# A new order for the mixers' steps and units in a two-layer hybrid backbone

## The chip, the cores and the metric

One core of a Trainium2 chip runs the whole program. The metric is device microseconds of one execution; the time given is the median of three.

## What is computed

One step of a two-layer backbone, for 128 context tokens and 256 latent tokens (T = 384 columns) of width 1024. Each layer projects its normed input `h` into the inputs of four mixers, weighs each mixer's projected output with sigmoid gates, adds the four, and goes on to an output projection and an MLP:

```python
h = _rms(x, norm_g[l, 0]) * (1.0 + sc1) + sh1
z = h @ w_in[l]
ya, ckv, kr = _mla(za, ...)            # A: latent attention
yb = _chunk_mlp(zb, ...)               # B: gated unit over chunks of 128 positions
yc, st = _mlstm(zc, ...)               # C: the cell, a matrix memory read in both directions
yd, kd, vd = _diff_attn(zd, ...)       # D: differential attention
br = jnp.einsum('blnw,nwd->blnd', jnp.stack([ya, yb, yc, yd], axis=2), w_branch[l])
gates = jax.nn.sigmoid(h @ w_merge[l] + b_merge[l]).reshape(B, L, N_BRANCH, D_MODEL)
y = jnp.sum(gates * br, axis=2) @ w_out[l]
```

In the cell the head outputs are normed and multiplied with another sigmoid:

```python
h = _rms(h, head_norm.reshape(H_C, DH_C)).reshape(B, L, D_C)
out = (jax.nn.sigmoid(o.astype(jnp.float32)) * h).astype(z.dtype)
```

## The kernel before

Activations lie with channels on the 128 partitions and the 384 tokens in the columns. Every large weight comes in blocks of 128 by 1024 and is split into two parts of fewer bits: `whi` by a cast on ScalarE (L117), `wlo` by a subtraction on VectorE (L119). The inputs are split the same way, into `hh` and `hl`. A *unit* is the work with one weight block on TensorE: 24 matmuls of 384 columns (`mm3`, L350 to L352) in most units, 36 of 256 columns in those that compute values with tokens on the partitions (`vproj`, L403 to L405). Results go to PSUM, which has four tiles called `mm` for units and four called `px` for everything smaller; each pool gives its tiles out in turn, so that a new use waits until the last reader of the old one is done.

`mix_plan` lists the units of a layer's mixing part in the order of their weights: five units for the cell's queries, keys and gate rows (MISC), two for the gated unit's `u` (BU), then values of the cell (CV), values of the gated unit (BV), the cell's output gate (CO), queries and keys of D (DQ, DK), and then four branches. A branch has twice four merge units (M0 to M7), whose sigmoids make the gates on ScalarE, and a branch unit (BR00 and BR01 in branch 0) after each four. The branch unit multiplies the mixer's output with its weights; VectorE multiplies four result blocks with the gates and, from the second branch on, adds them to `acc` (L1103 to L1106). Between branch 0 and branch 1 stand the values of D (DV) and the inputs of A (AQ, AKV). In layer 0 no work of a previous layer runs into this part. In layer 1 the part before it, here called the head, has computed the first units while it was still norming and scaling its input; `zb` and `zs` (L1543, L1544) are its results copied out of PSUM.

The mixers themselves are generators. `slot()` stands ahead of every unit: it orders loads and casts, runs each living generator as far as its next `yield` (`pump`), and then issues the due `wlo` subtractions and the jobs kept for that index. So the order on each engine is the order in which Python writes it, and every engine works through its own queue in that order. A generator is started by `spawn`; `finish` runs one to its end, which is what a branch does with its mixer before its branch unit. `C` is the cell (`mlstm`, L765), `B` the gated unit (`gmlp`, L746), `D` differential attention (`diff`), `A0` and `A` latent attention.

Names that the steps use: L775 are the cell's first products, which transpose the gate rows `grow` made by L1033. L411 spreads rows of the split operands `zq` and `mts` over partitions. L919 to L922 read the cell; L950 makes its new state; L966 sums squares for its last norm, L427 to L439 and L970, L971 are that norm's steps on VectorE. L754 are the gated unit's products, which read `qi`. In D, L642 are the scores, L601 and L602 the maximum and its scaling, L647 to L650 the weights of the softmax, L571 their transposes. L1172 and L1179 sum squares for A's norms.

Of the kernel before, what the change touches and what calls it, by code (L numbers as in the profile page):

```python
# [40 lines left out]
class Builder:  # L41
# [704 lines left out]
    def gmlp(self, l, vn, ub, wst, vb):  # L746
        nc = self.nc
        yh, yl = self.y_tiles(1)
        for b in range(2):
# [15 lines left out]
    def mlstm(self, l, grow, qc, km, kp, so):  # L765
# [96 lines left out]
        mask0()  # L862
        yield

        hbuf = s1([128, 2, T], "s3")
# [68 lines left out]
        for b in range(2):  # L934
            prev = None
            for hf in range(2):
                for d in range(2):
                    heads(b, hf, d, prev)
                    prev = (hf, d)
                    yield  # L940
            read(b, 0, prev)
            yield
            read(b, 1, None)
            if b == 0:
                nc.gpsimd.dma_start(self.c0, io["c0"][l, :, :, 1])
            yield
        for d in range(2):
            ps = self.px_tile()
# [26 lines left out]
    @staticmethod  # L975
    def mix_plan():
        w = lambda a, n: list(range(a, a + n))
        o = w(U_MISC, 5) + w(U_BU, 2) + w(U_CV, 2) + w(U_BV, 2) + w(U_CO, 2)
        for n in range(4):
            if n == 0:  # L980
                o += w(U_DQ, 4)
            if n == 1:
                o += w(U_DV, 5)
            for p in range(2):
                o += w(U_MERGE + 8 * n + 4 * p, 4) + w(U_BR + 2 * n + p, 1)
        return o

    def mix_phase(self, l, head):
# [60 lines left out]
        for j in range(len(head.units), len(fns)):  # L1049
            fns[j][0](fns[j][1], self.fm(l, self.mix_plan()[j], hh, hl), None)  # L1050
        for t, ps in enumerate(self.vproj(l, U_CV, hh, hl)):
            nc.scalar.copy(self.vcx[:, t].rearrange("p b (q e) -> p b q e", e=64)[:, :, 0:3:2, :],
                           ps.rearrange("p (b q e) -> p b q e", b=2, e=64))
        so = s1([128, 2, T], "s3")
        self.spawn("C", self.mlstm(l, grow, qc, km, kp, so))

# [10 lines left out]
        self.spawn("B", self.gmlp(l, vn, ub, wst, vb))  # L1067
        for b, ps in self.fm_pair(l, U_CO, hh, hl):
            self.sigmoid(so[:, b, :], ps)

        acc = self.hp.tile([128, KC, T], F32, tag="acc", name="acc")

        def branch(n, name):
            br = BR_ORDER[n]
            for part in range(2):
                gates, held = [], []
                for b in range(4 * part, 4 * part + 4):
                    held.append((b, self.fm(l, U_MERGE + n * 8 + b, hh, hl)))
                    if b % 2:
                        for bb, ps in held:  # L1080
                            g = mx.tile([128, T], F32, tag="g", name="g", bufs=4)
                            self.sigmoid(g, ps, bias=par[:, P_BM + br * 8 + bb:P_BM + br * 8 + bb + 1])
                            gates.append(g)
                        held = []
                self.finish(name)
                yh, yl = self.y[br]
# [10 lines left out]
                for j in range(4):  # L1097
# [4 lines left out]
                    if n == 0:  # L1102
                        nc.vector.tensor_tensor(acc[:, b, :], ps[:, :T], gates[j], ALU.mult)  # L1103
                    else:
                        nc.vector.tensor_tensor(gates[j], ps[:, :T], gates[j], ALU.mult)
                        nc.vector.tensor_tensor(acc[:, b, :], acc[:, b, :], gates[j], ALU.add)  # L1106
                    if end:
                        nc.scalar.copy(mh[:, b, 0:T], acc[:, b, :])
                        for k in late:
                            nc.vector.tensor_tensor(ml[:, k, 0:T], acc[:, k, :], mh[:, k, 0:T].bitcast(F32), ALU.subtract)  # L1110
                        late = [b]
                        if j == 1:
                            self.prefetch(len(self.split_w) + 1)
                if end:
                    nc.vector.tensor_tensor(ml[:, b, 0:T], acc[:, b, :], mh[:, b, 0:T].bitcast(F32), ALU.subtract)
                    self.low_parts()
            if n == 3:
                return mh, ml
# [18 lines left out]
        for b in range(2):  # L1137
# [5 lines left out]
            self.spawn("R", operand(self.kscr, b, kd, "ks", 512))  # L1143
        branch(0, "B")

        vd = s1([128, 4, 256], "vd")
        dma(vd[:, 1, :], io["xdv"][l])

        for t, ps in enumerate(self.vproj(l, U_DV, hh, hl)):
            nc.scalar.copy(vd[:, (0, 2, 3)[t], :], ps)  # L1150
        nc.gpsimd.dma_start(io["o_dv"][l], vd[:, 0, :])
        self.spawn("D", self.diff(l, stacks, vd))

# [15 lines left out]
        def latent():  # L1169
            ss = self.px_tile()  # L1170
            for i in range(2):
# [4 lines left out]
            for i in range(2):  # L1176
                nc.vector.scalar_tensor_tensor(zq[i], zq[i], par[:, P_QN + i:P_QN + i + 1], rs, ALU.mult, ALU.mult)
            ss = self.px_tile()
            nc.tensor.matmul(ss[:, :T], self.ones, sqk, start=True, stop=True)  # L1179
# [551 lines left out]
```

## Time and profile before

| | |
|---|---|
| median of three runs | 1407.64 us (1407.39 to 1408.38) |
| the profiled execution | 1410.98 us, its span 1409.2 us |
| TensorE busy | 1345.1 us, 95% of the span |
| VectorE busy | 943.1 us, 67% |
| ScalarE busy | 750.4 us, 53% |
| chain that ended last | TensorE 79%, VectorE 11%, ScalarE 5% |
| mixing part of layer 0, of layer 1 | 64 to 395 us, 764 to 1070 us |

The profile's "idle" is time in which an engine had nothing to run, with the instruction that ended it. TensorE's idle time is what the program could lose or win; idle time of the others costs nothing by itself. TensorE's clock has two levels here, 2.4 GHz (1.00 in the rows) and 1.2 GHz (0.50).

### The profile page before, as it was taken

Reading aid. Unit: us, or ns where it says so; the run is one execution under the profiler, and the core shown is the slowest. Engines: PE = TensorE matmul, PEld = TensorE weight load, DVE = VectorE, ACT = ScalarE, POOL = GpSimd, SP = SyncE. Lnnn points to the kernel's source line nnn. Section 1 sums busy time; section 2 is a strip of 40 time slices with the busy share of each in tenths; the row PEclk is TensorE's granted clock in tenths of the full one; section 3 lists DMA queues with packets and bytes.
Section 4 is the critical chain, followed back from the end, with each engine's and each line's share of the span. In section 5 each row is a group of like instructions: output and inputs, shape, how many; then the busy total and the mean of one; then the engine's idle time right before and its main releaser. Section 6 shows DMA issues by size and latency. Waiting matters only on the chain.

```text
span 1409.2 us, 20419 instructions
## 1 busy us (share of the span) xinstructions
PE 1345.1 (95%) x7722; PEld 1256.7 (89%) x7722; DVE 943.1 (67%) x1831; ACT 750.4 (53%) x1378; POOL 68.9 (5%) x128
## 2 busy tenths in 40 slices
PE   5999998999999999999999899899999999999995
PEld 2888887887998999999979899898989899999995
DVE  5557767865556777898777877786655676236544
ACT  4544756756455662264357467576745565235431
POOL 0101111100000000000001020210000000000000
PEclk9999999999999999999999999999999999999998
DMA  9355546445253447766745363542434443433331
GB/s 377 125 180 164 167 146 172 127 135 209 90 175 125 165 144 230 232 214 198 251 153 187 98 168 103 139 126 90 158 96 165 135 135 118 132 125 120 120 105 45
DMA packets 63090, 216.38 MB, mean 154 GB/s; under 512 B 7888, under 2 KB 11152, under 8 KB 62608
## 3 DMA queue, kind: packets, MB, share of 16 engines
q1 hardware_dynamic: 51552, 187.53, 40.2%
q0 software_dynamic: 10288, 25.51, 6.4%
q10 hardware_dynamic: 1152, 2.04, 0.4%
q8 instruction: 61, 1.00, 0.3%
q14 instruction: 37, 0.30, 0.1%
HBM read 207.27 MB, written 7.77 MB: 153 GB/s over the span
## 4 chain that ended last, share of the span: by engine, by line
PE 79%; DVE 11%; ACT 5%; issue 4%; DMA 1%; POOL 0%; SPq 0%; DVEq 0%; ACTq 0%; POOLq 0%
PE mm L350 22%; PE mm L351 22%; PE mm L352 22%; PE px L281 2%; DVE wlo L119 2%; PE mm L403 1%; ACT whi L117 1%; PE px L463 1%; PE mm L405 1%; PE mm L404 1%; DVE s L926 1%; PE px L589 1%; ACT L69 1%; PE px L727 1%; DVE yr L490 1%
## 5 line engine op out<-in xcount | busy, mean ns | idle before, releaser
L350 PE MATMUL mm<-hh,whi 128*128 128x384 f32 (+1 forms) x1344 | 469.8, 350 | 5.5 <-ACT hh L1505 2.9
L351 PE MATMUL mm<-hl,whi 128*128 128x384 f32 (+1 forms) x1344 | 458.5, 341 | 1.8 <-DVE hl L1510 1.8
L352 PE MATMUL mm<-hh,wlo 128*128 128x384 f32 (+1 forms) x1344 | 457.1, 340 | 0.0
L117 ACT CAST whi<-raw 128x1024 fp32r<-128x1024 f32 x268 | 279.2, 1047 | 259.8 <-PE mm L351 143.6
L119 DVE TENSOR_TENSOR wlo<-raw,whi 128x1024 fp32r<-128x1024 f32 x268 | 325.1, 1221 | 136.8 <-ACT whi L117 136.4
L350 PEld LDWEIGHTS mm<-hh,whi 128*128 128x128 f32 x1344 | 255.8, 190 | 31.7 <-issue 13.6
L351 PEld LDWEIGHTS mm<-hl,whi 128*128 128x128 f32 x1344 | 256.1, 191 | 5.2 <-DVE hl L1510 2.3
L352 PEld LDWEIGHTS mm<-hh,wlo 128*128 128x128 f32 x1344 | 255.9, 190 | 0.1
L351 PE MATMUL mm<-fl,whi 128*128 128x384 f32 x512 | 173.0, 338 | 0.0
L352 PE MATMUL mm<-fh,wlo 128*128 128x384 f32 x512 | 172.6, 337 | 0.0
L350 PE MATMUL mm<-fh,whi 128*128 128x384 f32 x512 | 172.4, 337 | 0.0
L352 PEld LDWEIGHTS mm<-fh,wlo 128*128 128x128 f32 x512 | 96.2, 188 | 0.0
L350 PEld LDWEIGHTS mm<-fh,whi 128*128 128x128 f32 x512 | 96.2, 188 | 0.0
L351 PEld LDWEIGHTS mm<-fl,whi 128*128 128x128 f32 x512 | 96.2, 188 | 0.0
L338 DVE SCALAR_TENSOR_TENSOR ce<-raw,cb 128x1024 f32<-128x1024 f32 x64 | 78.1, 1221 | 0.8
L69 ACT ACT_TABLE_LOAD x56 | 71.8, 1283 | 3.1 <-issue 2.2
L1250 DVE TENSOR_TENSOR f<-mm,rs 128x384 f32<-128x384 f32 x64 | 35.5, 555 | 50.6 <-PE mm L352 50.5
L82 ACT ACTIVATE g<-mm,par 128x384 f32<-128x384 f32 x64 | 36.5, 581 | 44.1 <-PE mm L352 43.6
L1256 ACT ACTIVATE f<-f,zs 128x128 f32<-128x128 f32 (+1 forms) x128 | 51.1, 446 | 11.5 <-DVE zs L1252 11.4
L74 ACT ACTIVATE p<-px,sm 128x384 f32<-128x384 f32 (+1 forms) x72 | 36.6, 510 | 30.1 <-DVE sm L602 29.8
L403 PE MATMUL mm<-whi,hh 128*128 128x256 f32 x144 | 44.1, 306 | 6.8 <-DVE acc L1103 5.1
L427 DVE TENSOR_SCALAR rv<-px 128x384 f32<-128x384 f32 x20 | 11.1, 557 | 54.2 <-ACT ry L78 54.2
(333 smaller groups left out, 1799.8 us busy)
## 6 DMA issues: line engine op xcount, KB each, us to landing
raw<-wm SPq DMA_DIRECT2D x268, 512.0 KB, 3.9
raw<-wmod SPq DMA_DIRECT2D x36, 512.0 KB, 3.8
raw<-wmodr SPq DMA_DIRECT2D x32, 512.0 KB, 4.3
graw<-wmod SPq DMA_DIRECT2D x16, 512.0 KB, 10.0
graw<-wmod POOLq DMA_DIRECT2D x12, 512.0 KB, 5.9
ks<-kscr POOLq DMA_DIRECT2D x24, 128.0 KB, 4.7
qm<-qscr POOLq DMA_DIRECT2D x24, 96.0 KB, 4.9
kscr<-ks POOLq DMA_DIRECT2D x4, 512.0 KB, 3.7
```

The source lines that it names most:

```text
L69: self.nc.scalar.preload_act_table_set(name)
L74: self.nc.scalar.activation(out, in_, AF.Exp, **kw)
L82: self.nc.scalar.activation(out, in_, AF.Sigmoid, **kw)
L117: nc.scalar.copy(hi, raw)
L119: self.lows[i] = lambda lo=lo, raw=raw, hi=hi: nc.vector.tensor_tensor(lo, raw, hi.bitcast(F32), ALU.subtract)
L338: nc.vector.scalar_tensor_tensor(e[0], now["raw"], 1.0, cb[c], ALU.mult, ALU.mult, accum_out=now["red"][:, n % 4, c:c + 1])
L350: nc.tensor.matmul(ps, wh[:, off:off + 128], xh, start=first, stop=False)
L351: nc.tensor.matmul(ps, wh[:, off:off + 128], xl, start=False, stop=False)
L352: nc.tensor.matmul(ps, wl[:, off:off + 128], xh, start=False, stop=last)
L403: nc.tensor.matmul(ps, hh[:, kk, sl], wh[:, c], start=(kk == 0), stop=False)
L1250: nc.vector.tensor_tensor(f, ps[:, :T], head.rs, ALU.mult)
L1256: nc.scalar.activation(f[:, a:b], f[:, a:b], AF.Relu, bias=shift[:, c:c + 1])
```

## The change

It is one edit of the order with five parts. (1) The cell is spawned before its value units CV, so its first step stands ahead of CV0, and the output gate's units CO with their sigmoids come before BV. (2) Three `yield`s are added: at the start of the gated unit, in the cell behind `mask0` and before its state output. (3) The values of D are computed as a function that branch 0 calls in its second half, behind the gates of M4 to M7 and ahead of `finish("B")` and BR01; D is spawned there. (4) The sums of A's norms use an `mm` tile where they used a `px` tile. (5) The gates of a half branch are one tile of four blocks. In branches 1 and 2 and in the first half of branch 3 the four adds into `acc` become one add of 128 by 1536, issued in the next slot; the last half keeps its four.

```diff
     def gmlp(self, l, vn, ub, wst, vb):
         nc = self.nc
+        yield
         yh, yl = self.y_tiles(1)
...
         mask0()
         yield
+        yield
...
             yield
+        yield
         for d in range(2):
             ps = self.px_tile()
...
-        o = w(U_MISC, 5) + w(U_BU, 2) + w(U_CV, 2) + w(U_BV, 2) + w(U_CO, 2)
+        o = w(U_MISC, 5) + w(U_BU, 2) + w(U_CV, 2) + w(U_CO, 2) + w(U_BV, 2) + w(U_DQ, 4)
         for n in range(4):
-            if n == 0:
-                o += w(U_DQ, 4)
             if n == 1:
-                o += w(U_DV, 5)
+                o += w(U_AQ, 3)
             for p in range(2):
-                o += w(U_MERGE + 8 * n + 4 * p, 4) + w(U_BR + 2 * n + p, 1)
+                o += w(U_MERGE + 8 * n + 4 * p, 4) + (w(U_DV, 2) if (n, p) == (0, 1) else []) + w(U_BR + 2 * n + p, 1)
...
+        so = s1([128, 2, T], "s3")
+        self.spawn("C", self.mlstm(l, grow, qc, km, kp, so))
         for t, ps in enumerate(self.vproj(l, U_CV, hh, hl)):
...
-        so = s1([128, 2, T], "s3")
-        self.spawn("C", self.mlstm(l, grow, qc, km, kp, so))
+        for b, ps in self.fm_pair(l, U_CO, hh, hl):
+            self.sigmoid(so[:, b, :], ps)
...
-        for b, ps in self.fm_pair(l, U_CO, hh, hl):
-            self.sigmoid(so[:, b, :], ps)
...
+                if between and part == 1:
+                    between()
                 self.finish(name)
...
-                        nc.vector.tensor_tensor(gates[j], ps[:, :T], gates[j], ALU.mult)
-                        nc.vector.tensor_tensor(acc[:, b, :], acc[:, b, :], gates[j], ALU.add)
+                        nc.vector.tensor_tensor(gates[:, j, :], ps[:, :T], gates[:, j, :], ALU.mult)
                     if end:
+                        nc.vector.tensor_tensor(acc[:, b, :], acc[:, b, :], gates[:, j, :], ALU.add)
...
+                elif n:
+                    quarter = acc[:, 4 * part:4 * part + 4, :]
+                    self.jobs[self.index] = [lambda q=quarter, g=gates: nc.vector.tensor_tensor(q, q, g, ALU.add)]
...
-        branch(0, "B")
-
-        vd = s1([128, 4, 256], "vd")
-        dma(vd[:, 1, :], io["xdv"][l])
-
-        for t, ps in enumerate(self.vproj(l, U_DV, hh, hl)):
-            nc.scalar.copy(vd[:, (0, 2, 3)[t], :], ps)
-        nc.gpsimd.dma_start(io["o_dv"][l], vd[:, 0, :])
-        self.spawn("D", self.diff(l, stacks, vd))
+
+        def values():
+            vd = s1([128, 4, 256], "vd")
+            dma(vd[:, 1, :], io["xdv"][l])
+            for t, ps in enumerate(self.vproj(l, U_DV, hh, hl)):
+                nc.scalar.copy(vd[:, (0, 2, 3)[t], :], ps)
+            dma(io["o_dv"][l], vd[:, 0, :])
+            self.spawn("D", self.diff(l, stacks, vd))
+
+        branch(0, "B", values)
...
-            ss = self.px_tile()
+            ss = self.mm_tile()
```

The last pair stands twice in `latent`. On TensorE, at the start of layer 1's mixing part, before (the L350 family with `px` is the head's last product, L290 a piece of the modulation, L403 to L405 the value unit CV0):

```order
L351 MATMUL px<-pl,whi 128x386
L352 MATMUL px<-ph,wlo 128x386
L290 MATMUL px<-C,ms 128x128 x4
L403 MATMUL mm<-whi,hh 128x256
L404 MATMUL mm<-whi,hl 128x256
L405 MATMUL mm<-wlo,hh 128x256
```

and after:

```order
L351 MATMUL px<-pl,whi 128x386
L352 MATMUL px<-ph,wlo 128x386
L290 MATMUL px<-C,ms 128x128 x4
L776 MATMUL px<-C,s_7423 128x128 x3
L403 MATMUL mm<-whi,hh 128x256
L404 MATMUL mm<-whi,hl 128x256
L405 MATMUL mm<-wlo,hh 128x256
```

The cell's first products, L775 before and L776 now, moved from behind both CV units to the place ahead of the first.

On TensorE in layer 1, around the cell's first transposes of `zq`, before:

```order
L351 MATMUL mm<-hl,whi 128x384
L352 MATMUL mm<-hh,wlo 128x384
L411 MATMUL px<-zq,identr 128x384
L411 MATMUL px<-zq,pairs 128x256
L350 MATMUL mm<-hh,whi 128x384
```

and after:

```order
L351 MATMUL mm<-hl,whi 128x384
L352 MATMUL mm<-hh,wlo 128x384
L411 MATMUL px<-zq,identr 128x384
L411 MATMUL px<-zq,pairs 128x256
L755 MATMUL px<-s_7408,qi 64x128 x6
L350 MATMUL mm<-hh,whi 128x384
```

The gated unit's first products (L754 before, L755 now) come behind them; before they stood four units ahead of them. Between the cell's scores (L828) and these transposes stood one unit, DQ1; now there are two, BV1 and DQ0.

On VectorE in layer 1, around the four `acc` products of BR01 (L1103 before, L1104 now), before:

```order
L119 TENSOR_TENSOR wlo<-raw,whi 128x1024
L1103 TENSOR_TENSOR acc<-mm,g 128x384 x4
L119 TENSOR_TENSOR wlo<-raw,whi 128x1024
L427 TENSOR_SCALAR rv<-px 128x384
L119 TENSOR_TENSOR wlo<-raw,whi 128x1024
L436 TENSOR_TENSOR rt<-ry 128x384
```

and after:

```order
L427 TENSOR_SCALAR rv<-px 128x384
L601 TENSOR_REDUCE sm<-px 128x1
L602 TENSOR_SCALAR sm<-sm 128x1
L601 TENSOR_REDUCE sm<-px 128x1
L602 TENSOR_SCALAR sm<-sm 128x1
L119 TENSOR_TENSOR wlo<-raw,whi 128x1024
L1104 TENSOR_TENSOR acc<-mm,g 128x384 x4
L436 TENSOR_TENSOR rt<-ry 128x384
```

The first step of the cell's norm (L427) and D's first two maxima now stand ahead of the products, and the norm's other steps directly behind them.

## Rows read from the trace of the kernel before

**Rows 1.** The page: busy us, share of the span, instructions of TensorE.

```profile
PE 1345.1 (95%) x7722; PEld 1256.7 (89%) x7722; DVE 943.1 (67%) x1831; ACT 750.4 (53%) x1378; POOL 68.9 (5%) x128
```

**Rows 2.** TensorE's waits, 64 to 395 us: total us, times, longest.

```profile
PE px L411 <- DVE zq L419: 2.8, 1, 2.8
PE px L1179 <- ACT s L576: 2.4, 1, 2.4
PE mm L403 <- DVE acc L1103: 2.2, 1, 2.2
...
PE px L919 <- ACT s L74: 1.2, 1, 1.2
...
PE px L754 <- DVE qi L1065: 0.9, 1, 0.9
PE px L919 <- DVE s L930: 0.6, 1, 0.6
```

**Rows 3.** TensorE's waits, 764 to 1070 us.

```profile
PE mm L403 <- DVE acc L1103: 2.8, 1, 2.8
PE px L642 <- ACT p L74: 2.5, 3, 0.9
PE px L411 <- DVE zq L419: 2.2, 1, 2.2
PE mm L403 <- ACT vcx L1052: 1.6, 1, 1.6
PE px L754 <- DVE qi L1065: 1.0, 1, 1.0
```

**Rows 4.** Two stretches: us, busy (instructions), PEclk, DMA share, GB/s.

```profile
117.90:121.30 3.40, 3.40 (x11) 3.40 (x12) 3.35 (x9) 1.53 (x5) 0.36 (x1) 0.50 0.07 19
882.50:889.30 6.80, 6.08 (x28) 6.08 (x29) 3.15 (x6) 0.00 (x0) 0.00 (x0) 0.50 0.49 159
```

**Rows 5.** Timeline, start of layer 1's mixing: start, us, instruction.

```profile
764.60 0.36 PE L403 MATMUL mm<-whi,hh 128*128 128x256 f32 x1
...
770.53 0.62 ACT L1033 ACTIVATE s<-zb,par 128x384 f32<-128x384 f32 x1
...
772.39 0.15 DVE L1544 COPY zs<-px 128x2 f32<-128x2 f32 x1
...
773.89 0.49 PE L775 MATMUL px<-C,s 128*128 128x128 f32 x3
```

**Rows 6.** Timeline, layer 1, BR01 to AKV: products, norm, softmax, casts.

```profile
882.60 1.95 DVE L1103 TENSOR_TENSOR acc<-mm,g 128x384 f32<-128x384 f32 x4
...
890.37 1.05 ACT L117 CAST whi<-raw 128x1024 fp32r<-128x1024 f32 x1 [8.31 <-PE mm L404]
891.44 0.58 ACT L78 ACTIVATE ry<-px,eps 128x384 f32<-128x384 f32 x1
892.05 0.56 DVE L427 TENSOR_SCALAR rv<-px 128x384 f32<-128x384 f32 x1 [6.37 <-ACT ry L78]
892.52 1.22 DVE L119 TENSOR_TENSOR wlo<-raw,whi 128x1024 fp32r<-128x1024 f32 x1
893.66 0.55 DVE L436 TENSOR_TENSOR rt<-ry 128x384 f32<-128x384 f32 x1
...
897.22 0.56 DVE L419 TENSOR_TENSOR s<-ry,s 128x384 fp32r<-128x384 f32 x1 [0.58 <-ACT s L416]
...
898.18 0.28 DVE L601 TENSOR_REDUCE sm<-px 128x1 f32<-128x128 f32 x1
...
900.24 0.51 PE L642 MATMUL px<-ks,qm 96*128 96x384 f32 x2
...
904.12 0.16 DVE L647 RECIPROCAL sm<-sm 128x2 f32<-128x2 f32 x1
...
905.33 0.30 PE L571 MATMUL px<-C,p 128*128 128x128 f32 x1 [0.35 <-DVE p L650]
...
921.04 1.28 ACT L69 ACT_TABLE_LOAD   x1
```

More of the change, by code (lines that the diff above doesn't have):

```diff
@@ L1067, in mix_phase, with branch @@
         self.spawn("B", self.gmlp(l, vn, ub, wst, vb))
-        for b, ps in self.fm_pair(l, U_CO, hh, hl):
-            self.sigmoid(so[:, b, :], ps)
         acc = self.hp.tile([128, KC, T], F32, tag="acc", name="acc")
-        def branch(n, name):
+        def branch(n, name, between=None):
             br = BR_ORDER[n]
             for part in range(2):
-                gates, held = [], []
+                gates, held = mx.tile([128, 4, T], F32, tag="g", name="g"), []
                 for b in range(4 * part, 4 * part + 4):
@@ L1080, in branch @@
                         for bb, ps in held:
-                            g = mx.tile([128, T], F32, tag="g", name="g", bufs=4)
-                            self.sigmoid(g, ps, bias=par[:, P_BM + br * 8 + bb:P_BM + br * 8 + bb + 1])
-                            gates.append(g)
+                            self.sigmoid(gates[:, bb % 4, :], ps, bias=par[:, P_BM + br * 8 + bb:P_BM + br * 8 + bb + 1])
                         held = []
+                if between and part == 1:
+                    between()
                 self.finish(name)
@@ L1102, in branch @@
                     if n == 0:
-                        nc.vector.tensor_tensor(acc[:, b, :], ps[:, :T], gates[j], ALU.mult)
+                        nc.vector.tensor_tensor(acc[:, b, :], ps[:, :T], gates[:, j, :], ALU.mult)
                     else:
-                        nc.vector.tensor_tensor(gates[j], ps[:, :T], gates[j], ALU.mult)
-                        nc.vector.tensor_tensor(acc[:, b, :], acc[:, b, :], gates[j], ALU.add)
+                        nc.vector.tensor_tensor(gates[:, j, :], ps[:, :T], gates[:, j, :], ALU.mult)
                     if end:
+                        nc.vector.tensor_tensor(acc[:, b, :], acc[:, b, :], gates[:, j, :], ALU.add)
                         nc.scalar.copy(mh[:, b, 0:T], acc[:, b, :])
@@ L1177, in latent @@
                 nc.vector.scalar_tensor_tensor(zq[i], zq[i], par[:, P_QN + i:P_QN + i + 1], rs, ALU.mult, ALU.mult)
-            ss = self.px_tile()
+            ss = self.mm_tile()
             nc.tensor.matmul(ss[:, :T], self.ones, sqk, start=True, stop=True)
```

## The prediction

> **What bounds the kernel now.** I read the head of the page first, then TensorE's list of waits, by layer, then the granted clock of the stretches behind the longest waits, then the order of events at the places that the change touches. TensorE is busy for 95% of the span [rows 1], and it does the same instructions after the change. So the change can only pay by ending waits of TensorE, with what they do to its clock, or cost by making new ones. It touches only the two token-mixing stretches (64 to 395 us in layer 0, 764 to 1070 us in layer 1). There the waits are few and have names: in layer 0 the transposes L411 for `zq` (2.8 us), the latent sum L1179 (2.4), the first value unit L403 for the branch sum `acc` (2.2) [rows 2]; in layer 1 `acc` again (2.8), `zq` (2.2), the copy of the cell's values `vcx` (1.6), the gated unit's `qi` (1.0) [rows 3]. Behind five of these (both `zq`, both `acc`, and L1179) stands a stretch at a granted clock of 0.50, 1.2 GHz where 2.4 is the upper level: 3.4 us with TensorE busy throughout behind four of them, of which one row stands, and 6.8 us, 6.08 of it busy, behind layer 1's `acc` [rows 4]. Work at half clock takes twice its time, so they cost 1.7 us four times and 3.0 once. Behind the 1.6 us wait for `vcx` no such stretch stands.
>
> **The change part by part.** The sum is made against the profiled execution, 1410.98 us (its span is 1409.2, so 1.8 lie around it); that is 3.3 above the median of 1407.64, and I carry the difference over unchanged. I count a wait that ends as its row, plus what the clock behind it cost.
>
> *The cell starts two units sooner, with pauses.* Its first product (L775) now stands ahead of the value unit CV0; the pause after `mask0` leaves a further unit between the scores and the transposes L411 that read their split `zq`. The order shows two units there instead of one, and a unit is 905.33 - 0.35 - 900.75 = 4.2 us [rows 6], more than either `zq` wait. Both go: -(2.8 + 1.7) and -(2.2 + 1.7). The gated unit starts behind its own pause: its two waits for `qi` go, -0.9 and -1.0. Its three products of the next slot stand behind a vector step that now runs beside a change of ScalarE's function table (1.28 us, [rows 6]), and the second batch behind a split on ScalarE. Not shown in the trace; between 0 and two waits of the size of today's (2.0). I take 1.1 a layer.
>
> *The price of it is in layer 1.* In layer 0 the gate rows that L775 reads are ready long before CV0 is reached. In layer 1 the head, which norms the layer's input, is still at work when TensorE arrives. L775 needs the gate rows of L1033, begun at 770.53, and a PSUM tile that the copy L1544 gives back at 772.39 + 0.15 = 772.54. CV0 begins at 764.60 and needs neither; L775 stands at 773.89, behind both value units, and waits for nothing [rows 5]. Put ahead of CV0 it holds TensorE from 764.60 to 772.5: +7.9. VectorE's and ScalarE's queues before those two instructions hold only the head's own work, so nothing there comes sooner. The wait for `vcx` goes, since ScalarE catches up meanwhile: -1.6. Behind 7.9 us of waiting I expect a half-clock stretch, +1.7 (up to 3.4).
>
> *Values ahead of the branch.* DV0 no longer follows branch unit BR00/BR01 and its `acc` products, so the `acc` waits go: -(2.2 + 1.7) and -(2.8 + 3.0). But the same VectorE work now meets BR01. The cell's last norm and the first softmax of the attention D both fall between BR01 and AKV. From the end of DV1 (t = 0), with durations from [rows 6]: ScalarE does a short copy and a cast of 1.05 (to 1.5), a table load (2.75), the logarithm L78 (3.3). VectorE's L427 waits for that (3.9), then come two maxima with their scalings (4.75), one weight split of 1.22 (5.9) and the four `acc` products, begun at 5.9 instead of 1.7 and done at 7.85. AQ0 follows BR01 and takes the first tile that they free, at 6.4. The norm's steps L436 to L971 take 3.0 (10.85), ScalarE's split 0.5, L419 0.5, L427 0.5, four short steps 1.1 (13.5). TensorE, through with AQ0 at 10.6, waits 3 us for them at L571, then for the next exponent, and begins AQ1 at 15.0. One more round of that kind (softmax, weight split, the second half's norm) puts AKV at 23.0, where three units from 0.65 with the small products between them would put it at 16.0. So +7.0 a layer. What before loses here besides goes into it: L571 0.35 [rows 6] and one L642 of 0.9 [rows 3] in layer 1, the same two with 0.3 and 0.8 in layer 0: -1.2 and -1.1. In layer 0 the order of the three engines at this place is the same. Bounds: +1.1 (VectorE has idle time during DV0 and DV1, and the table load is done there) and +8.7 (a half-clock stretch of 1.7 behind the 3 us).
>
> *The latent sum in another PSUM pool.* L1179 waits for a `px` tile that a copy must free; the `mm` tiles show no such wait in this stretch. -(2.4 + 1.7) in layer 0, nothing in layer 1.
>
> *Cell reads* (L919, layer 0: 1.2 and 0.6): they wait for ScalarE and VectorE, and the cell's steps lie at other units now. Half goes: -0.9.
>
> *Adds by four blocks.* Four products of 384 columns take 1.95 us; one add over 1536 columns should take 1.7 to 1.8, by the 1.22 of 1024 columns (both in [rows 6], an estimate). The saving is under 0.3 us for each of the five adds in a layer (ten in all), on VectorE in branches 1 to 3, where TensorE's waits in both lists are 0.9 or less. Nothing on the path. Were that cover gone, the whole add would cost 1.8 once.
>
> Layer 0: -4.5 - 0.9 + 1.1 - 3.9 + 7.0 - 1.1 - 4.1 - 0.9 = -7.3. Layer 1: +7.9 + 1.7 - 1.6 - 3.9 - 1.0 + 1.1 - 5.8 + 7.0 - 1.2 = +4.2. Together -3.1: 1407.9 for the profiled execution, 1404.5 against the median. Its own range goes from 1400 (the `qi` successors and half of one stretch cost nothing) to 1409 (a longer clock stretch behind L775, the stretches at 8.7, less 1 us where they overlap).
>
> **A rule on the clock.** Of the sum, the clock alone is -9.8 (the five stretches of [rows 4]) + 1.7 = -8.1; without it the waits come to +5.0. The Trainium skill ("TensorE: Matmul & The Clock Gate", Part 1) holds that how long the cold part lasts varies from run to run and that a model should not be fitted to it, the ramp being under 1% of a typical kernel. Against that the rows show five named waits with a slow stretch behind each, together 0.7% of this span, more than the effect forecast; so I keep the terms. By the rule the sum would be 1412.6, which is close to the second rival.
>
> **The rivals.** *One, much faster:* the walk through BR01 to AKV is wrong, VectorE uses its free time in DV0 and DV1 and the stretch costs only what it costs before (1.1 and 1.2). Then -3.1 - 5.9 - 5.8 = -14.8: 1392.8. For it: during the value unit of before VectorE is busy for 3.15 us of 6.80 only [rows 4]. Against: L427 stands first in its queue and waits for ScalarE, and the four products stand behind it. *Two, slower:* the clock gives nothing back. Each layer's stretch has two waits of 2 to 3 us, as long as those that had a half-clock stretch behind them; with L775's that makes five new stretches for five that go, 5 x 1.7 - 9.8 = -1.3 instead of -8.1: +3.7, 1411.3, and 1412.6 at a balance of zero. It decides from a balance of -2.2 upwards. Against: while VectorE is what TensorE waits for, work at half clock eats the next wait and costs less. *Three, no difference:* only the stretches are dearer, 8.7 in each layer: -3.1 + 3.4 = +0.3, 1407.9; the places of the waits change and their sum does not.
>
> **How the numbers follow.** A measurement of this kernel tells 0.2%, about 2.8 us, from no change. The forecast has 0.38, rival one 0.20, rival three 0.25, rival two 0.17. The forecast lies only 0.3 beyond that bound, but the uncertain bounds under it (L571's rounds, the `qi` successors) reach further down than up, and I give 0.28 of its 0.38 to faster, 0.08 to the same, 0.02 to slower. Rival one is faster throughout; rival three goes 0.03, 0.17, 0.05; rival two 0, 0.02, 0.15. Together 0.51 faster, 0.27 the same, 0.22 slower. The range of 8 in 10 takes half of rival one and nearly all of rival two: 1394 to 1413.
>
> **What would show it.** In the trace of the changed kernel: L775 (now numbered L776) of layer 1 with TensorE idle before it for over 7 us, released by `zs`; no wait for `zq`, none for `acc` at a value unit, none at the latent sum; instead L571 behind L650 for 2 to 3 us twice a layer, at AQ0's and AQ1's ends; in layer 0 a mixing stretch shorter by about 7 us, in layer 1 longer by about 4. The prediction is wrong if L775 starts by 767 (the head is then not what it waits for), if AKV begins less than 18 us after the end of DV1, or if more than three half-clock stretches stand in the two mixing stretches.

## The result

The changed kernel takes 1415.62 us (1414.83 to 1415.99, four runs), the kernel before 1407.52 in the same runs: a ratio of 1.0056, interval 1.0034 to 1.0078. It is 8.1 us slower, where 3.1 us faster was forecast with a range up to 1413. Its profiled execution took 1415.76 us, so it is a typical one; that of the kernel before (1410.98) was not, as two further looks at that kernel show below.

The page of the changed kernel, busy us of each engine (against [rows 1]):

```profile
PE 1344.7 (95%) x7722; PEld 1258.6 (89%) x7722; DVE 938.5 (66%) x1801; ACT 748.6 (53%) x1378; POOL 68.5 (5%) x128
```

TensorE is as busy as before, though its work at half clock was to fall by 8.1 us. Its waits in layer 0's mixing part, 64 to 395 us (total us, times, longest), against [rows 2]:

```profile
PE px L571 <- DVE p L650: 4.2, 3, 2.5
PE px L642 <- ACT p L74: 2.2, 3, 0.8
PE px L695 <- ACT ptp L576: 1.9, 1, 1.9
PE px L727 <- ACT ptp L576: 1.5, 1, 1.5
PE px L411 <- DVE s L932: 0.7, 1, 0.7
PE px L755 <- DVE qi L1068: 0.6, 1, 0.6
```

and in layer 1's, 764 to 1070 us, against [rows 3]:

```profile
PE px L776 <- DVE zs L1549: 7.8, 1, 7.8
PE px L571 <- DVE p L650: 4.6, 3, 2.5
PE px L642 <- ACT p L74: 2.2, 3, 0.8
PE px L695 <- ACT ptp L576: 1.9, 1, 1.9
```

Every wait that was to go is gone: both `zq`, both `acc`, the latent sum, `vcx`. L776 waits 7.8 us where 7.9 was worked out. New and not forecast are L695 in both layers and L727 in layer 0. The sums of the two full lists are 12.6 us (before 14.3) and 18.1 (before 11.1), +5.3 together. That is nearly the whole difference between the two profiled executions, +4.8; TensorE's busy time adds -0.4.

The stretches at half clock in the changed kernel's mixing parts (us, TensorE busy, PEclk, DMA share, GB/s), against [rows 4]:

```profile
208.50:211.90 3.40, 3.17 (x10) 0.50 0.31 73
269.90:273.30 3.40, 3.40 (x12) 0.50 0.00 0
324.50:327.90 3.40, 3.40 (x16) 0.51 0.47 117
768.30:775.10 6.80, 4.01 (x19) 0.50 0.74 234
901.40:904.80 3.40, 3.40 (x12) 0.50 0.64 197
959.40:962.80 3.40, 3.40 (x12) 0.50 0.00 0
```

Six stretches at 1.2 GHz where the kernel before had five. They stand behind the new waits: L571, L695, L727 in layer 0, L776, L571, L695 in layer 1. TensorE is busy for 20.8 us in them, and half of that, 10.4 us, is what the lower clock costs; the five of the kernel before cost 9.8.

Where the time lies, in us, measured between the same places of TensorE's program, found in every profile by the count of its instructions: the beginning of layer 0's first cell value unit (72.2 us in the first profile of before; in the changed kernel the cell's first products stand at that count), a place behind layer 0's mixing (395.6), the end of layer 1's head (762.1), a place behind layer 1's mixing (1070.7), TensorE's last matmul (1394.7). Two further looks at the kernel before and one at the changed one are in it, and three experiments:

| | start | layer 0 | between | layer 1, with the end of its head | behind |
|---|---|---|---|---|---|
| before, first | 72.2 | 323.4 | 366.5 | 308.6 | 324.1 |
| before, second | 69.2 | 325.1 | 366.8 | 307.1 | 322.5 |
| before, third | 72.6 | 321.1 | 365.2 | 307.1 | 322.5 |
| changed, first | 71.8 | 320.5 | 368.3 | 314.9 | 324.0 |
| changed, second | 72.0 | 322.2 | 368.1 | 315.2 | 324.1 |
| D's values back | 71.5 | 312.0 | 366.6 | 307.9 | 324.0 |
| values ahead, D later | 72.7 | 315.6 | 368.2 | 311.2 | 324.0 |
| values back, cell of layer 1 as before | 71.4 | 312.0 | 366.7 | 305.5 | 324.0 |

By the means of these profiles the changed kernel is 9.2 us longer: layer 0 gained 1.9 us and layer 1 lost 7.4, so +5.6 in the parts that the change touches. The other 3.6 lie in parts with the same instructions in the same order.

### The profile page after: what moved, and what is told of

It is laid out like the page before. It is cut to its first block, busy times and chain, and to the rows that moved or that the text cites. A ratio compares the mean times of both kernels' runs of the same rounds, so it can differ in the third digit from the quotient of the medians.

```text
span 1414.0 us, 20375 instructions
## 1 busy us (share of the span) xinstructions
PE 1344.7 (95%) x7722; PEld 1258.6 (89%) x7722; DVE 938.5 (66%) x1801; ACT 748.6 (53%) x1378; POOL 68.5 (5%) x128
## 4 chain that ended last, share of the span: by engine, by line
PE 82%; DVE 10%; ACT 4%; issue 1%; DMA 1%; DVEq 0%; SPq 0%; ACTq 0%
PE mm L350 23%; PE mm L351 23%; PE mm L352 23%; PE px L281 2%; DVE wlo L119 1%; PE px L463 1%; ACT whi L117 1%; PE mm L403 1%; PE mm L405 1%; PE mm L404 1%; PE px L727 1%; ACT L69 1%; PE px L589 1%; DVE rt L437 1%; DVE ry L439 1%
## 5 line engine op out<-in xcount | busy, mean ns | idle before, releaser
L350 PE MATMUL mm<-hh,whi 128*128 128x384 f32 (+1 forms) x1344 | 470.4, 350 | 5.5 <-ACT hh L1510 2.9
L350 PEld LDWEIGHTS mm<-hh,whi 128*128 128x128 f32 x1344 | 256.6, 191 | 30.7 <-issue 14.0
L350 PE MATMUL mm<-fh,whi 128*128 128x384 f32 x512 | 172.4, 337 | 0.0
L350 PEld LDWEIGHTS mm<-fh,whi 128*128 128x128 f32 x512 | 96.2, 188 | 0.0
L69 ACT ACT_TABLE_LOAD x56 | 71.8, 1283 | 3.1 <-issue 2.2
L350 PE MATMUL mm<-s,whi 128*128 128x384 f32 x128 | 44.9, 351 | 0.0
L601 DVE TENSOR_REDUCE sm<-px 128x1 f32<-128x384 f32 (+1 forms) x72 | 33.2, 461 | 15.9 <-PE px L727 13.4
```

The source lines that it names most:

```text
L69: self.nc.scalar.preload_act_table_set(name)
L350: nc.tensor.matmul(ps, wh[:, off:off + 128], xh, start=first, stop=False)
L601: nc.vector.tensor_reduce(m[:, j:j + 1], ps[:, :N], AX.X, ALU.max)
```

## The experiments

Each experiment undoes or isolates a part of the change; "before" in a ratio is the kernel before, run in the same batch. Theories at the outset: the lump (the one large add comes at a bad moment), the phase (D starts one unit earlier and its steps meet other work), the place (D's values ahead of BR01), the head (L776 in layer 1), and the clock.

**Single adds again.** The four adds of the kernel before in the changed one:

```diff
                         nc.vector.tensor_tensor(gates[:, j, :], ps[:, :T], gates[:, j, :], ALU.mult)
+                        nc.vector.tensor_tensor(acc[:, b, :], acc[:, b, :], gates[:, j, :], ALU.add)
...
-                elif n:
-                    quarter = acc[:, 4 * part:4 * part + 4, :]
-                    self.jobs[self.index] = [lambda q=quarter, g=gates: nc.vector.tensor_tensor(q, q, g, ALU.add)]
```

> The changed kernel with the four single adds per half branch back in place of the one add over 1536 columns; all else as changed. Theory one, the lump: the whole add of 1.75 us stands on VectorE directly ahead of D's first norm and softmax and makes L571 late (waits of 1.2 us in layer 0, 1.7 in layer 1 at the start of branch 2, each followed by half clock). Then those two waits go and with them about 3 us, up to 6.5 if the two half-clock stretches behind go too: 1409 to 1412.5 us against 1415.6. Rival, the phase: D's steps stand one unit earlier against the sigmoids, and that alone makes these waits. Then L571 still waits over 1 us there and the time stays within 1.5 us of 1415.6.

1409.68 us (1406.5 to 1412.94), ratio to before 1.0022 (1.0008 to 1.0036): 5.9 less than the changed kernel. The place is shown by the timeline of the changed kernel in layer 1, at the start of branch 2 (start, us, instruction, idle before and what ended it):

```profile
946.55 1.75 DVE L1120 TENSOR_TENSOR acc<-acc,g 128x1536 f32<-128x1536 f32 x1
948.22 0.55 DVE L436 TENSOR_TENSOR rt<-ry 128x384 f32<-128x384 f32 x1
...
952.38 0.35 DVE L650 SCALAR_TENSOR_TENSOR p<-p,sm 128x128 f32<-128x128 f32 x1
...
952.88 0.30 PE L571 MATMUL px<-C,p 128*128 128x128 f32 x1 [1.71 <-DVE p L650]
...
954.76 1.28 ACT L69 ACT_TABLE_LOAD   x1
...
956.06 1.05 ACT L82 ACTIVATE g<-mm,par 128x384 f32<-128x384 f32 x2
...
957.00 1.04 ACT L117 CAST whi<-raw 128x1024 fp32r<-128x1024 f32 x1
...
957.93 0.28 ACT L576 COPY ptp<-px 128x128 f32<-128x128 f32 x1
...
958.26 1.83 PE L695 MATMUL px<-zq,s 128*128 128x384 f32 x4 [1.91 <-ACT ptp L576]
```

The add of 1.75 us stands straight ahead of D's norm, a chain of VectorE and ScalarE, and the weights (L650) come behind that: L571 waits 1.7 us. Without the lump that wait is 0.6 in layer 1, and in layer 0, where it was 1.2, it is gone. Part of it comes back later in the layer: layer 0's wait for `ptp` at L727 grows from 1.5 to 2.9 us. The lower half of the rows is another matter and stays: a table load, two sigmoids and a cast stand ahead of the small copy L576 on ScalarE, which frees the `px` tile that L695 needs.

**D's values behind the branch again.** The third part undone, the rest as changed:

```diff
-                if between and part == 1:
-                    between()
...
-        branch(0, "B", values)
+        branch(0, "B")
+        values()
```

> The changed kernel with D's values computed behind branch 0 again, and D spawned there; all else as changed. Theory one, the phase: with D one unit later the waits at its second half (L571 and L695, about 3 us more than before in each layer, with a half-clock stretch each) go, and the stretch from BR01 to AKV (7.3 and 7.1 us with its clock) is exchanged for the waits for acc and its successors of before (5.7 and 7.9). About 1407 to 1410 us. Rival, the lump: the add over 1536 columns makes the later waits; they stay, and the time is 1414 to 1416.

1396.93 us (1395.47 to 1398.34), ratio 0.9922 (0.9900 to 0.9945): 18.7 less than the changed kernel, far more than either theory gave, and faster than the kernel before. Its waits in layer 1 from 764 us (L776 lies ahead of that):

```profile
PE px L642 <- ACT p L74: 2.5, 3, 0.9
PE px L571 <- DVE p L650: 1.6, 1, 1.6
PE px L755 <- DVE qi L1068: 0.6, 1, 0.6
PE px L755 <- ACT qi L74: 0.6, 1, 0.6
```

L695 and L727 are down to 0.3 or less in both layers, the whole add is still there, and no value unit waits for `acc`: the cell's earlier reads have already ended that wait, without the values' move. Layer 0 is shorter by 9.4 us and layer 1 by 7.1 (table, against the mean of the two looks at the changed kernel).

**Only D later.** Values ahead of BR01 as changed, D spawned behind BR01:

```diff
-            self.spawn("D", self.diff(l, stacks, vd))
+            self.vd = vd
 
         branch(0, "B", values)
+        self.spawn("D", self.diff(l, stacks, self.vd))
```

> The changed kernel with D's values still computed ahead of BR01, but D itself spawned behind BR01, one unit later, as before against the merge units that follow. Theory one, D's phase: what the values' new place costs comes from D's steps lying one unit earlier, where they meet the cell's last norm and later the sigmoids and the whole add; then the waits at L571 behind AQ0, at L695 and at L571 in branch 2 go and the time is near that of the values behind the branch: 1396 to 1402. Rival, the values' place: the units themselves, ahead of BR01, push BR01's products into the cell's norm; then waits of over 2 us stay between BR01 and AKV and the time is above 1408.

1406.11 us (1402.22 to 1407.77), ratio 0.9994 (0.9981 to 1.0006): 9.5 less than the changed kernel and 9.2 more than with the values back. Neither theory alone, and neither expected range was hit: by these medians D's phase is half of the price, the place the other half. What stays, between BR01 and AKV in layer 1:

```profile
PE px L571 <- DVE p L650: 2.3, 1, 2.3
PE px L642 <- DVE rv L427: 1.3, 1, 1.3
```

**The values ahead alone.** The same third part put into the kernel before.

```diff
+                if between and part == 1:
+                    between()
...
-        branch(0, "B")
+        branch(0, "B", values)
```

> The kernel before with one part of the change alone: D's values computed in branch 0 ahead of BR01, D spawned there. Theory one, this part is what makes the change slower: the waits for acc at the value unit go (2.2 and 2.8 us, with their half clock), but L571 waits 2 to 3 us behind AQ0 in both layers and D's later steps wait at L695 (1.9 us) in both, as in the changed kernel: 3 to 7 us slower than before, 1410 to 1414. Rival, the cell's pauses make the collision: without them the cell's norm is done by BR01 and D alone gives VectorE little to do; then no wait over 1.5 us stands between BR01 and AKV and the time is 3 to 8 us below before.

1416.25 us (1415.16 to 1416.55), ratio 1.007 (1.0052 to 1.0087): 10.5 slower than before. Waits in layer 0:

```profile
PE px L411 <- DVE zq L419: 2.8, 1, 2.8
PE px L571 <- DVE p L650: 2.1, 2, 1.6
PE px L642 <- ACT p L74: 1.9, 3, 0.8
PE px L695 <- ACT ptp L576: 1.9, 1, 1.9
PE px L1182 <- ACT ptp L576: 1.9, 1, 1.9
PE px L727 <- ACT ptp L576: 1.7, 1, 1.7
```

That is more than either theory gave. `acc` is off the list in both layers; L571, L695 and L727 have taken its place; the latent sum (here L1182) waits for its `px` tile as before. The waits rose by 3.6 us over both layers, and the mixing parts, measured as in the table, by 4.2 (325.8 and 309.2 against the means 323.2 and 307.6). The rest lies outside them, as in the changed kernel, and isn't explained by this move.

**The cell of layer 1 as before.** Spawned behind its values there, without its two pauses; D's values ahead:

```diff
-        self.spawn("C", self.mlstm(l, grow, qc, km, kp, so))
+        if l == 0:
+            self.spawn("C", self.mlstm(l, grow, qc, km, kp, so))
...
+        if l:
+            self.spawn("C", self.mlstm(l, grow, qc, km, kp, so))
```

> The changed kernel with the cell of layer 1 spawned behind its values and without the cell's two added pauses there; layer 0 as changed. Theory: the wait at L776 of layer 1 (7.8 us and 3.4 us of half clock behind it) goes, and the waits for vcx (1.6) and zq (2.2, with 1.7 of half clock) come back: 5.5 to 6 us less, about 1410. Rival: the head's work is what TensorE waits for in any order, and the next unit that needs it waits as long; then over 5 us of waiting stand within the first five units of layer 1's mixing and the time stays above 1413.

1409.49 us (1407.22 to 1414.28), ratio 1.0024 (1.0008 to 1.0040): 6.1 less than the changed kernel, as expected. The 7.8 us are gone and `zq` waits 2.1 again; the wait for `vcx`, which was expected back, is not there, and the next transposes wait 1.8 instead.

**The latent sum in an `mm` tile, alone**, in the kernel before (both places):

```diff
-            ss = self.px_tile()
+            ss = self.mm_tile()
```

> The kernel before with the sums of A's norms in an mm tile; nothing else changed. Theory: the wait at L1179 in layer 0 (2.4 us and 1.7 us of half clock behind it) goes: about 4 us less than before. Rival: a short wait comes at the next unit that needs an mm tile or at the next step that needs the norm, and the half-clock stretch with it; then the difference to before is under 1.5 us.

1403.41 us (1399.6 to 1408.2), ratio 0.9971 (0.9956 to 0.9985): 3.6 less than before, as expected. Its profiled run, 1399.6, is the first sign about the clock: the waits for `zq` and `acc` ahead of the latent sum are those of [rows 2], 2.8 and 2.3, but nothing at half clock stands behind them (the granted clock is 1.00 there), and TensorE is busy 12 us less with the same instructions:

```profile
PE 1332.8 (95%) x7722; PEld 1245.7 (89%) x7722; DVE 943.6 (68%) x1831; ACT 749.7 (54%) x1378; POOL 69.0 (5%) x128
```

**Values back and single adds.** Both edits above.

> The changed kernel with both D's values and the four single adds back in their old places. Theory one: with D one unit later no wait of TensorE stands behind the whole add, so single adds change nothing: 1395 to 1399, as with the values back alone (1396.9). Rival, the lump costs in any phase: 2 us or more below 1396.9.

1396.33 us (1393.92 to 1399.17), ratio 0.993 (0.9907 to 0.9954), against 1396.93 with the whole adds: no difference. The lump costs in the changed kernel's phase only.

**Values back, late cell in layer 1**, first with all pauses, then without the one before the state output:

```diff
+        if l:
+            self.spawn("C", self.mlstm(l, grow, qc, km, kp, so))
```

> The changed kernel with D's values back behind branch 0, and in layer 1 the cell spawned behind its values, all pauses kept. Theory: the wait at L776 (7.8 us, 3.4 of half clock behind it) goes; zq keeps two units and doesn't wait; vcx waits 1.6 at most: 8 to 11 us less than 1396.9, so 1386 to 1389. Rival: the cell ends two units later and its last norm now meets D's first softmax, as in the changed kernel; then waits of 2 to 3 us at L571 come back in layer 1 and half of the gain goes: 1391 to 1394.

> As the kernel above (values back, late cell in layer 1) but without the pause before the cell's state output in layer 1, so that the cell ends one unit earlier. Theory: same gain at L776, and the cell's last norm clear of D's first softmax: 1386 to 1389, up to 2 us below the kernel above. Rival: the norm's place makes no difference, the two are within 1 us of each other.

1404.0 us (1402.53 to 1405.0), ratio 0.9985 (0.9970 to 1.0000), and 1400.97 (1398.8 to 1404.33), ratio 0.9964 (0.9951 to 0.9976). Both theories missed: it is 7 and 4 us *slower* than with the wait at L776. The first one's waits in layer 1:

```profile
PE mm L350 <- DVE acc L1105: 3.8, 1, 3.8
...
PE px L826 <- ACT qi L74: 2.9, 1, 2.9
```

Two units later, the cell's first read lies over branch unit BR00, and its `acc` products stand on VectorE behind the read's reciprocal (L928, 2.55 us). These waits take the place of the one at L776: up to AKV's first matmul, found by the count, layer 1 takes 143.4 and 143.0 us, where the kernel with the values back takes 142.9. The loss lies behind that place, 170.7 and 168.0 against 165.0. There the cell's last norm now stands on VectorE ahead of D's softmax, as the rival said, and L571 waits; in the second kernel, from AKV on:

```profile
PE px L571 <- DVE p L650: 1.9, 1, 1.9
```

**Values back, the cell's first step one unit later in layer 1**, no pause behind `mask0` there:

```diff
+        if l:
+            yield
         U, L = C[:, C_U:C_U + 128], C[:, C_L:C_L + 128]
```

> The changed kernel with D's values back, and in layer 1 the cell's first step one unit later (at CV1) and no pause behind mask0, so that all its later steps stay where they were. Theory: the wait at L776 falls from 7.8 us to 3.3 to 3.6, with no more than 1.7 us of half clock behind it; zq has one unit less and waits about 2 us with 1.7 of half clock: 1393 to 1396 against 1396.9. Rival, the wait is passed on: L776 waits less and the next steps that need its result wait as much more; within 1 us of 1396.9.

1400.35 us (1397.07 to 1401.37), ratio 0.9953 (0.9937 to 0.9969). That is 3.4 more than with the values back alone, and outside both expected ranges. Most of the wait is passed on:

```profile
PE px L778 <- DVE zs L1551: 2.9, 1, 2.9
...
PE px L411 <- DVE zq L419: 2.3, 1, 2.3
PE px L755 <- ACT s L840: 2.0, 1, 2.0
```

The first step waits 4.9 us less, and the two that follow 3.6 more (2.3 and 2.0, where the kernel with the values back alone has one wait of 0.6); both stand ahead of 6.8 us at half clock. The layer comes out 0.5 us longer (308.4 against 307.9); where the rest of the 3.4 lies is open, but 1.5 of it is in the part between the layers (368.1 against 366.6), which no edit touches.

**Values back, the cell of layer 1 as before.** The two edits together.

> The changed kernel with D's values back, and the cell of layer 1 started behind its values without its two added pauses, as in the kernel before. Theory, the parts add: the cell's late start in layer 1 took 6.1 us from the changed kernel, so 1390 to 1392 here. Rival, they don't: with the reads one unit later the products of BR01 stand behind the cell's last read again, DV0 waits for acc (2.8 us and 1.7 to 3.4 of half clock) as in the kernel before: 1395 to 1399.

1395.95 us (1395.22 to 1397.25), ratio 0.9929 (0.9910 to 0.9949): the shortest median of all, but within 1 us of the values back alone, and their ranges overlap, so the parts don't add. The rival's reason shows:

```profile
PE mm L403 <- DVE acc L1107: 2.8, 1, 2.8
PE px L642 <- ACT p L74: 2.4, 3, 0.9
PE px L411 <- DVE zq L419: 2.1, 1, 2.1
```

With the reads one unit later, `acc` waits 2.8 us again: in this kernel it is the cell's start and pauses that end that wait.

**The same kernels again**, unedited: the kernel before twice more, the changed kernel once more.

> The kernel before, unchanged, for a second look at the clock. Theory one, the waits set the clock: the same waits (zq 2.8 and 2.2 us, acc 2.2 and 2.8, the latent sum 2.4) have the same half-clock stretches behind them as in the first profile, 1.7 us four times and about 3.0 once; TensorE busy 1345 us again, within 2. Rival, a wait of 2 to 3 us has half clock behind it in some runs only: the waits are the same within 0.1 us, some of the five stretches are missing, and TensorE's busy time and the span are shorter by as much, 2 to 12 us.

> The kernel before, for a third look. Theory one: the parts outside the mixing vary between the values of the first two profiles (62.2 and 59.2 us up to layer 0's mixing, 229.5 and 227.9 behind layer 1's), the mixing parts stay within 2 us of 323.4 or 325.1 and of 308.6 or 307.1, and what varies is the granted clock behind the same waits. Rival: another of the waits in the mixing parts changes by over 0.5 us from run to run, and the time with it.

> The changed kernel, unchanged, for a second look. Open is how much of the 8.1 us lies outside the two mixing parts. Theory one, the parts outside vary from run to run in either kernel and average out: up to layer 0's mixing 59 to 63 us, layer 0's mixing 320.5, layer 1's 315, each within 2. Rival, the changed kernel is always slow in the parts outside: 61.8 us up to layer 0's mixing, 63.6 between 700 and 762 us and 229.4 behind layer 1's mixing again, each within 0.5.

1406.94, 1404.85 and 1418.03 us, one execution each. The kernel before, second look: its page, then two of its waits over the whole run, then the stretch behind layer 0's wait for `zq`; the last fence is the third look's stretch behind that same wait of 2.8 us:

```profile
PE 1339.3 (95%) x7722; PEld 1251.6 (89%) x7722; DVE 943.7 (67%) x1831; ACT 750.9 (53%) x1378; POOL 69.0 (5%) x128
```

```profile
PE px L411 <- DVE zq L419: 5.0, 2, 2.8
...
PE px L1179 <- ACT s L576: 3.1, 1, 3.1
```

```profile
118.00:121.40 3.40, 2.84 (x16) 1.00 0.50 154
```

```profile
118.20:121.60 3.40, 3.40 (x12) 0.53 0.07 19
```

The same wait, once with half clock behind it and once without. Nearly all waits are the same within 0.1 us in all three looks (the latent sum goes from 2.1 to 3.1, and the second look alone has two more of 0.6 and 0.5), yet TensorE's busy time is 1345.1, 1339.3 and 1339.3. The rival holds: such a wait has half clock behind it in some runs only. The changed kernel had 1344.7 and, in its second look, 1348.3.

The stretches at half clock in the mixing parts, by look; their cost is half of TensorE's busy time in them:

| | stretches | TensorE busy in them, us | cost, us |
|---|---|---|---|
| before, first | 5 | 19.7 | 9.8 |
| before, second | 4 | 15.6 | 7.8 |
| before, third | 4 | 13.1 | 6.6 |
| changed, first | 6 | 20.8 | 10.4 |
| changed, second | 6 | 28.6 | 14.3 |

So the profile on which the prediction rests had the most of it, but no look had fewer than four stretches, and the changed kernel had six in both.

Of the parts outside the mixing, the table shows the rival for the changed kernel: within 0.5 us in both looks, and 2 us more between the layers than before, where a half-clock stretch near 728 us stands in both of its profiles and in none of the three of before. Why it is steady there, with the same instructions, was not found.

## Why the prediction was wrong

**The step that failed: what D's earlier start costs behind AKV, put at nothing.** The walk went from BR01 to AKV and ended there, and what lay behind had no term but the latent sum's. AKV's first matmul splits each layer's part in two (us; the changed kernel does five of D's small products more ahead of it):

| | layer 0 up to AKV | behind it | layer 1 up to AKV | behind it |
|---|---|---|---|---|
| forecast | -3.2 | -4.1 | +4.2 | 0 |
| before, mean of three looks | 149.0 | 174.3 | 143.9 | 163.8 |
| changed, mean of two | 145.0 | 176.4 | 148.1 | 167.0 |
| difference | -4.0 | +2.1 | +4.2 | +3.2 |
| D's values back, one look | 140.4 | 171.6 | 142.9 | 165.0 |

Up to AKV each layer comes out within 1 us of its terms. Behind it layer 0 was to lose the latent sum's wait and became longer, and layer 1 was to stay: a miss of 9.4 us, which is more than the whole miss in the two mixing parts, 8.6. What is missing beyond that, to the 11.1 us between 1404.5 and 1415.62, lies outside these parts and in the base. D's steps move by one unit against the merge units' sigmoids and the large add, which stay where they are. In layer 1 that made L571 1.7, L642 0.8, L695 2.1 us at the start of branch 2, where before had 1.9 in all, and in layer 0 4.1 against 1.3, with L727 besides; three stretches at half clock stand behind these waits and cost 5.1 more. With its share between BR01 and AKV, D's phase is 9.5 us (the run with only D later). The add was "nothing on the path" with a price of 1.8 "were that cover gone": the cover was gone once a layer, and it cost 1.1 to 1.2 us of waiting at L571 each time; the run with single adds is shorter by 5.9 us in the median, of which the lists show 2.1 as waits.

**A second step: the clock's balance.** The prediction took -9.8 us for five half-clock stretches that go and +1.7 for one that comes; TensorE's busy time fell by 0.4. The five went. Six came, at 10.4 us: one behind L776 (2.0), one a layer behind L571 at AQ0's end (3.3 together), which took the place of second waits that the walk had paid for, and the three behind D's later steps. That the waits come to +5.3, where the terms without the clock say +5.0, is luck: the stretch from BR01 to AKV, put at 7.0 us of waiting a layer, has 4.4 and 4.3, and D's later steps have some 3 us a layer more than before. Rival two, "the clock gives nothing back", is near in its number (1411.3 to 1412.6), but three of the six stretches stand at waits that it didn't know of. One of the prediction's own signs of being wrong, more than three half-clock stretches in the mixing parts, was met.

The credit was also less sure than it looked, since it came from one execution: such stretches cost 9.8, 7.8 and 6.6 us in three looks. The Trainium skill ("TensorE: Matmul & The Clock Gate", Part 1) says of the warm-up that its cold part varies from run to run and that a model shouldn't be fitted to it. The three looks agree, for stretches in the middle of a kernel. The sum without the clock, 1412.6, lies 3.0 below the measured time, where the forecast lies 11.1 below.

**A third: the base.** "I carry the difference over unchanged": the 3.3 us between the profiled run of before and the median were not an offset of profiling. They were a run with more half clock: the two other looks, also profiled, took 1406.94 and 1404.85 us, with TensorE busy 5.8 us less. The changed kernel's profiled run lies 0.1 above its median. From the one profiled run to the other the time rose by 4.8 us; the other 3.3 of the 8.1 are this.

**A credit in the wrong place.** "DV0 no longer follows branch unit BR00/BR01 and its `acc` products, so the `acc` waits go." They went, and in the kernel before this move alone ends them too. But the run with the values back has none either, and the one that also has the cell of layer 1 as before has it again there: within the change, the cell's earlier start and pauses are enough. So the values' move bought nothing here and was priced at +2.0 net (14.0 of new waiting, 9.7 and 2.3 returned); alone it costs 10.5, with the rest of the change 18.7.

**What was right.** The sum of each layer up to AKV came within 1 us. L776: 7.8 us against 7.9, its half clock 2.0 (4.01 us busy at 0.50) against 1.7. The waits for `zq`, `vcx`, `qi` and the latent sum went as listed, `qi`'s successors are 1.2 a layer against 1.1, and the cell's reads wait 1.4 less against 0.9. The walk from BR01 to AKV in the changed kernel's layer 1, counted from the first product behind DV1 (L969), at 886.04:

```profile
886.04 0.81 PE L969 MATMUL px<-s,C 128*128 128x384 f32 x2
...
889.48 0.56 DVE L427 TENSOR_SCALAR rv<-px 128x384 f32<-128x384 f32 x1 [6.62 <-ACT ry L78]
...
891.86 1.94 DVE L1104 TENSOR_TENSOR acc<-mm,g 128x384 f32<-128x384 f32 x4
...
899.44 0.30 PE L571 MATMUL px<-C,p 128*128 128x128 f32 x1 [2.48 <-DVE p L650]
...
907.29 0.52 PE L571 MATMUL px<-C,p 128*128 128x128 f32 x3 [0.37 <-DVE p L650]
...
908.73 0.39 PE L350 MATMUL mm<-hh,whi 128*128 128x384 f32 x1
```

L427 at 3.4 (3.3 worked out), the products at 5.8 (5.9), L571 at 13.4 (13.5), AKV at 22.7 (23.0). The second wait at L571 was to be 2 to 3 us and is 0.4, because AQ1 ran at half clock meanwhile (901.40 to 904.80 us): time lost either way, as the second rival's counter-argument said. Layer 0 was to gain 7.3 and gained 1.9; layer 1 was to lose 4.2 and lost 7.4.

## What to carry to other kernels

When a stream of steps is shifted by one slot, walk it to its end against everything with a fixed place (sigmoid pairs, table loads, large adds): what was missed here lay up to two branches behind the edit. Price half clock on both sides by the same rows: where the waits that go have a slow stretch behind them, expect some behind the new waits too, or leave the clock out on both sides and count the waits alone. One profile shows where such stretches can stand, not that they will, so take several. And ask of each wait that a change ends which of its parts ends it; here the costly part was credited with what another part did as well, and without it the rest of the change is worth 10 us.

## What the runs showed of the hardware

- A wait of 2.8 us with the same instructions around it was followed by 3.4 us at 1.2 GHz in two looks and by none in another; over all kernels here, in which TensorE does the same 7722 matmuls, its busy time lay between 1332.8 and 1348.3 us.
- One add over 1536 columns takes 1.75 us; four products of 384 columns take 1.94. The saving of 0.2 us is less than the 1.1 to 1.2 us of waiting that its lump costs where it stands ahead of a chain.
- A wait taken from the head of a chain of steps can come back at the steps that need its result: 4.9 us off the cell's first step in layer 1, 3.6 us on at two later ones.
